# Scaling the softmax exponentials on VectorE instead of GpSimd, in a two-layer transformer block

## Chip, cores and metric

The kernel runs on one core of a Trainium2 chip. The metric is the device time of one execution in microseconds (us). The engines are TensorE (PE, with its weight loads as PEld), VectorE (DVE), ScalarE (ACT), GpSimd (POOL) and SyncE (SP, which issues nearly all DMAs). Each engine works through its own instructions in a fixed order; semaphores make one engine wait for another.

## What is computed

Two transformer layers on a sequence of 256 tokens with 1024 features, all in fp32. Each layer has a mixer with three kinds of attention (8 MLA heads, 4 "fox" heads with a forget-gate bias, 4 "moba" heads with a T5 bias) and a gated feed-forward part; both are modulated by columns computed from a condition vector.

```python
def dense_causal_attention(q, k, v, log_decay_cum=None):
    ...
        s = jnp.einsum('bhqd,bhkd->bhqk', q_i, k).astype(jnp.float32) * scale
        if log_decay_cum is not None:
            s = s + blk[2][..., None] - log_decay_cum[:, :, None, :]
        s = jnp.where(kpos[None, :] <= qpos[:, None], s, -jnp.inf)
        p = jax.nn.softmax(s, axis=-1)
        return jnp.einsum('bhqk,bhkd->bhqd', p.astype(v.dtype), v)

def reference(x, c, ...):
    c_act = jax.nn.silu(c)
    for l in range(DEPTH):
        mod = (c_act @ w_ada[l] + b_ada[l])[:, None, :]
        shift_a, scale_a, gate_a, shift_f, scale_f, gate_f = jnp.split(mod, 6, axis=-1)
        h = rmsnorm(x, g_mix_pre[l]) * (1.0 + scale_a) + shift_a
        y = hybrid_mixer(h, w_in[l], ..., g_group[l], w_out[l], t5_table)
        x = x + gate_a * rmsnorm(y, g_mix_post[l])
        h = rmsnorm(x, g_ffn_pre[l]) * (1.0 + scale_f) + shift_f
        x = x + gate_f * rmsnorm(swiglu(h, w_gate_up[l], w_down[l]), g_ffn_post[l])
    return x
```

## The kernel before, in words

Tokens lie on partitions in two tiles of 128, or on the free axis after a transpose. Every weight matrix streams from HBM in fp32 and is split into a high part `wh` (ScalarE, line 107) and a remainder `wl` (VectorE, line 108); a product is three matmuls (lines 153 to 155 and 175 to 177). The modulation matrices `adaw` are used up chunk by chunk in between, some by TensorE (line 299), some by VectorE as a product with row `crow` and a sum (line 277); the SyncE queue loads the next chunk into a buffer when VectorE or TensorE has left it (4 buffers).

In the mixer the 16 heads come as 8 pairs: four MLA pairs, two fox pairs, two moba pairs. For a pair TensorE computes the scores `s` (lines 500 and 502, one PSUM tile for each head), then for each head `softmax` runs. VectorE adds the mask or bias and takes the row minimum of the negated scores, once for the first 128 queries (128 keys, line 477) and once for the second (256 keys, line 479), into tile `e` of 128 x 384. ScalarE takes the two exponentials and their sums (lines 482 and 483). VectorE takes the reciprocals of the two sums (line 485). GpSimd multiplies the two parts of `e` by them (lines 486 and 487). Then TensorE transposes the three blocks of `e` into `pt` (line 493), ScalarE copies them to `pts` (line 495), and TensorE forms the head outputs `o` (line 521). A pair's transposes and outputs are issued one pair later for MLA and two pairs later for fox and moba (`DEPTH`), with projections and modulation chunks in between.

Each of the three groups then needs the sum of its squared outputs: `acc` is added on VectorE (line 527), summed over partitions by TensorE into `st` (line 461), turned into a factor on ScalarE (lines 463 and 464), applied on VectorE as `ov` (line 538), and split into `oH` and `oL`. The output projection `y` (lines 175 to 177, 96 matmuls a layer) takes `oH` and `oL` of eight 128-row pieces, the MLA pieces first and the moba pieces last. Its accumulators come from the same four PSUM buffers as the scores:

```python
def pa(name, n=512):
    return psum.tile([P, n], F32, tag="pa", bufs=4, name=name)
```

so `y` of the first token tile takes the buffers that the scores of the first moba pair held, and that of the second token tile those of the second moba pair. After `y` a norm follows (lines 385 to 454), then transposes `xT` (line 423) and the feed-forward part, whose matmuls are most of the time.

The order of the instructions on each engine is made by a scheduler of the framework from the code, with its own estimate of what each instruction takes. So a change in one line can move other instructions on all engines.

## Time and profile before

| | us |
|---|---|
| median of 3 runs | 661.24 (659.17 to 662.15) |
| the profiled execution, whole | 659.96 |
| its span, from the first to the last instruction | 658.2 |
| TensorE busy in the span | 630.1 |
| VectorE busy | 452.2 |
| ScalarE busy | 366.3 |
| GpSimd busy | 58.7 |

The granted clock of TensorE was 0.999 of full speed over the span. The two mixers with their attention lie at about 60 to 142 us and 353 to 450 us of the span; the feed-forward parts follow each of them. A row of the time line gives an instruction's start and duration, and in brackets how long its engine had been idle before it and what ended that; a row of the waits gives the sum, the count and the longest. Instructions of one engine overlap a little: the next one may start before the last one is recorded as over.

### The profile page before, as it was taken

What the parts mean: (1) busy time and instruction counts of PE and PEld (TensorE: products, weight loads), DVE (VectorE), ACT (ScalarE), POOL (GpSimd) and SP (SyncE); (2) the same over time, 40 slices, a digit from 0 to 9 for tenths busy, and PEclk for the clock granted to TensorE, in tenths of its full rate; (3) what the DMA queues carried; (4) which work ended last, traced back from release to release, by engine and by line L of the source; (5) the groups of instructions that cost most, each with busy time, mean ns of one, the idle gap of its engine ahead of it and who ended that gap; (6) DMA issues with size and microseconds to landing.
All of it is one profiled execution on the core that took longest, in us unless ns stands there. A gap on an engine that the chain in (4) does not pass through costs nothing.

```text
span 658.2 us, 11876 instructions
## 1 busy us (share of the span) xinstructions
PE 630.1 (96%) x4469; PEld 558.3 (85%) x4469; DVE 452.2 (69%) x892; ACT 366.3 (56%) x760; POOL 58.7 (9%) x95
## 2 busy tenths in 40 slices
PE   7998989999999999999999999999999999999996
PEld 5888776678999999999978997667999999999994
DVE  3878568878777777795668665957867854555443
ACT  5467577777644444444477765877754444444431
POOL 2000134400000000000011031420000000000000
PEclk9999999999999999999999999999999999999999
DMA  8988979654788998998834776724378665555511
GB/s 315 402 320 290 312 250 319 226 188 157 238 279 307 333 296 312 306 338 308 286 132 134 260 256 192 257 97 134 127 262 305 196 222 176 183 189 188 182 47 64
DMA packets 43337, 154.46 MB, mean 235 GB/s; under 512 B 5052, under 2 KB 5248, under 8 KB 43280
## 3 DMA queue, kind: packets, MB, share of 16 engines
q1 hardware_dynamic: 43008, 153.07, 68.1%
q8 instruction: 35, 0.57, 0.3%
q0 software_dynamic: 272, 0.63, 0.3%
q14 instruction: 22, 0.18, 0.1%
HBM read 152.60 MB, written 1.08 MB: 233 GB/s over the span
## 4 chain that ended last, share of the span: by engine, by line
PE 74%; DMA 10%; DVE 7%; ACT 3%; issue 2%; POOL 2%; SPq 1%; DVEq 0%; POOLq 0%; ACTq 0%
PE gu L153 11%; PE gu L154 11%; PE gu L155 11%; PE y L177 8%; PE y L175 8%; PE y L176 8%; DMA adaw<-in_w_ada_dram 5%; DVE wl L108 3%; PE o L521 2%; DMA raw_a<-in_w_a_dram 2%; DMA raw_b<-in_w_b_dram 2%; POOL rs L386 1%; PE pt L493 1%; ACT wh L107 1%; DVE x L454 1%
## 5 line engine op out<-in xcount | busy, mean ns | idle before, releaser
L108 DVE TENSOR_TENSOR wl<-raw_gu,wh 128x1024 fp32r<-128x1024 f32 (+1 forms) x100 | 108.5, 1095 | 70.3 <-ACT wh L107 69.9
L107 ACT ACTIVATE wh<-raw_gu 128x1024 fp32r<-128x1024 f32 (+1 forms) x100 | 94.3, 957 | 92.3 <-PE gu L154 66.7
L277 DVE CUSTOM_DVE_ANT_0 adaw<-adaw,crow 128x1024 f32<-128x1024 f32 x64 | 77.6, 1227 | 15.0 <-DMA adaw<-in_w_ada_dram 14.9
L153 PE MATMUL gu<-h0fL,wh 128*128 128x256 f32 x304 | 86.1, 283 | 0.0
L153 PE MATMUL gu<-h1fL,wh 128*128 128x256 f32 x304 | 86.1, 283 | 0.0
L154 PE MATMUL gu<-h1fH,wh 128*128 128x256 f32 x304 | 86.1, 283 | 0.0
L154 PE MATMUL gu<-h0fH,wh 128*128 128x256 f32 x304 | 86.0, 283 | 0.0
L155 PE MATMUL gu<-h1fH,wl 128*128 128x256 f32 x304 | 86.0, 283 | 0.0
L155 PE MATMUL gu<-h0fH,wl 128*128 128x256 f32 x304 | 85.9, 283 | 0.0
L107 ACT ACTIVATE wh<-raw_dn 128x1024 fp32r<-128x1024 f32 x44 | 46.6, 1060 | 57.5 <-issue 36.4
L108 DVE TENSOR_TENSOR wl<-raw_dn,wh 128x1024 fp32r<-128x1024 f32 x44 | 53.7, 1223 | 24.7 <-ACT wh L107 24.5
L176 PE MATMUL y<-wh,hid 128*128 128x512 f32 x176 | 69.6, 395 | 0.0
L175 PE MATMUL y<-wh,hid 128*128 128x512 f32 x176 | 69.5, 396 | 0.0
L177 PE MATMUL y<-wl,hid 128*128 128x512 f32 x176 | 69.5, 395 | 0.0
L154 PEld LDWEIGHTS gu<-h1fH,wh 128*128 128x128 f32 x304 | 58.2, 192 | 0.4
L154 PEld LDWEIGHTS gu<-h0fH,wh 128*128 128x128 f32 x304 | 58.2, 192 | 0.4
L153 PEld LDWEIGHTS gu<-h1fL,wh 128*128 128x128 f32 x304 | 58.2, 192 | 0.4
L153 PEld LDWEIGHTS gu<-h0fL,wh 128*128 128x128 f32 x304 | 58.2, 192 | 0.4
L155 PEld LDWEIGHTS gu<-h1fH,wl 128*128 128x128 f32 x304 | 58.2, 192 | 0.0
L155 PEld LDWEIGHTS gu<-h0fH,wl 128*128 128x128 f32 x304 | 58.2, 192 | 0.0
L386 POOL TENSOR_TENSOR rs<-rs,mhalf 128x1 f32<-128x1 f32 x16 | 11.1, 691 | 438.2 <-DVE rs L385 438.2
L177 PEld LDWEIGHTS y<-wl,hid 128*128 128x128 f32 x176 | 33.0, 188 | 8.0
(343 smaller groups left out, 1464.6 us busy)
## 6 DMA issues: line engine op xcount, KB each, us to landing
adaw<-in_w_ada_dram SPq DMA_DIRECT2D x96, 512.0 KB, 5.7
raw_gu<-in_w_gu_dram SPq DMA_DIRECT2D x88, 512.0 KB, 5.0
raw_dn<-in_w_dn_dram SPq DMA_DIRECT2D x44, 512.0 KB, 4.7
raw_out<-in_w_out_dram SPq DMA_DIRECT2D x16, 512.0 KB, 6.3
raw_b<-in_w_b_dram SPq DMA_DIRECT2D x12, 512.0 KB, 4.9
raw_a<-in_w_a_dram SPq DMA_DIRECT2D x8, 448.0 KB, 9.8
raw_uq<-in_w_uq_dram SPq DMA_DIRECT2D x4, 512.0 KB, 4.9
raw_vm<-in_w_vm_dram SPq DMA_DIRECT2D x4, 512.0 KB, 5.1
```

The lines of the kernel that those rows point to most:

```text
L107: ACT.activation(dst_h, src, AF.Copy)
L108: return DVE.tensor_tensor(dst_l, src, dst_h.bitcast(F32), op=ALU.subtract)
L153: chain(PE.matmul(ps, w[0], x[1], start=start, stop=False))
L154: chain(PE.matmul(ps, w[0], x[0], start=False, stop=False))
L155: chain(PE.matmul(ps, w[1], x[0], start=False, stop=stop))
L175: PE.matmul(ps, x[1], w[0], start=start, stop=False)
L176: PE.matmul(ps, x[0], w[0], start=False, stop=False)
L177: PE.matmul(ps, x[0], w[1], start=False, stop=stop)
L277: i = DVE.tensor_tensor_reduce(out=raws[u], in0=raws[u], in1=crow, op0=ALU.mult, op1=ALU.add, scale=1.0, scalar=0.0, accum_out=dst[:, u:u ...
L386: POOL.tensor_tensor(r, r, mhalf, op=ALU.pow)
L454: DVE.scalar_tensor_tensor(x[:, t, sl], ygs[n], r, x[:, t, sl], op0=ALU.mult, op1=ALU.add)
L521: PE.matmul(o[64 * u:64 * u + 64, lo:lo + n], v[:, u * 64:(u + 1) * 64], ps[u][:, i * P:i * P + n], start=i == 0, stop=i == 2, tile_positi ...
```

## The change

The two multiplications of each head go from GpSimd to VectorE, directly behind the reciprocal in the code. The tile, its parts and the factor stay as they are; the second multiplication by 1.0 inside the instruction goes.

```diff
         ri = wk.tile([P, 2], F32, tag="ri", bufs=4, name="ri")
         DVE.reciprocal(ri, sm)
-        POOL.tensor_scalar(e[:, 0:P], e[:, 0:P], ri[:, 0:1], 1.0, op0=ALU.mult, op1=ALU.mult)
-        POOL.tensor_scalar(e[:, P:3 * P], e[:, P:3 * P], ri[:, 1:2], 1.0, op0=ALU.mult, op1=ALU.mult)
+        for t, sl in ((0, slice(0, P)), (1, slice(P, 3 * P))):
+            DVE.tensor_scalar(e[:, sl], e[:, sl], ri[:, t:t + 1], None, op0=ALU.mult)
         return e
```

There are 32 heads in the two layers, so 64 instructions leave GpSimd's queue and 64 join VectorE's. They don't always stand directly behind their reciprocal there, and the scheduler has put other instructions into another order, on TensorE and ScalarE too. Three places follow.

VectorE in layer 0, second MLA pair, second head: from its reciprocal (tile `ri_1048`, of the exponentials `e_1041`) to the queries `qx_1121` of the third MLA pair. Before:

```order
L485 RECIPROCAL ri_1048<-sm_1045 128x2
L277 ISA adaw_1098,gcol_887<-adaw_1098,crow_110 128x1024
L277 ISA gcol_887 128x1
L108 TENSOR_TENSOR wl_826<-raw_out_823,wh_825 128x1024
L277 ISA adaw_1099,gcol_887<-adaw_1099,crow_110 128x1024
L277 ISA gcol_887 128x1
L806 TENSOR_TENSOR qx_1121<-qp_1120,qt_648 128x512
```

After:

```order
L277 ISA adaw_1098,gcol_887<-adaw_1098,crow_110 128x1024
L277 ISA gcol_887 128x1
L108 TENSOR_TENSOR wl_826<-raw_out_823,wh_825 128x1024
L485 RECIPROCAL ri_1048<-sm_1045 128x2
L277 ISA adaw_1099,gcol_887<-adaw_1099,crow_110 128x1024
L277 ISA gcol_887 128x1
L487 TENSOR_SCALAR e_1041<-e_1041,ri_1048 128x128
L487 TENSOR_SCALAR e_1041<-e_1041,ri_1048 128x256
L354 TENSOR_TENSOR gcol_887<-gcol_887,first_73 128x8
L806 TENSOR_TENSOR qx_1121<-qp_1120,qt_648 128x512
```

The reciprocal now stands behind one modulation chunk (`adaw_1098`) and one weight split, and another chunk (`adaw_1099`) stands between it and the two scalings; `qx` comes behind all of them.

VectorE in layer 0, around the reciprocals of the second fox pair (`acc<-acc,osq` is the sum of squares of the MLA group, `ov<-oc` its outputs, `e,mn<-s,mobab` the minima of the first moba pair). Before:

```order
L277 ISA adaw,ab_1221<-adaw,crow 128x1024
L277 ISA ab_1221 128x1
L485 RECIPROCAL ri<-sm 128x2 x2
L326 TENSOR_TENSOR ab_1221<-ab_1221,first 128x8
L477 ISA e,mn<-s,mobab 128x128
L477 ISA mn 128x1
L527 TENSOR_TENSOR acc<-acc,osq 128x256
L328 SCALAR_TENSOR_TENSOR ab_1221<-ab_1221,first 128x4
L479 ISA e,mn<-s,mobab 128x256
L479 ISA mn 128x1
```

After:

```order
L527 TENSOR_TENSOR acc<-acc,osq 128x256
L277 ISA adaw,ab_1221<-adaw,crow 128x1024
L277 ISA ab_1221 128x1
L485 RECIPROCAL ri<-sm 128x2 x2
L277 ISA adaw,ab_1221<-adaw,crow 128x1024
L277 ISA ab_1221 128x1
L487 TENSOR_SCALAR e<-e,ri 128x128
L487 TENSOR_SCALAR e<-e,ri 128x256
L487 TENSOR_SCALAR e<-e,ri 128x128
L487 TENSOR_SCALAR e<-e,ri 128x256
L538 SCALAR_TENSOR_TENSOR ov<-oc,first,ocr 128x256 x2
L326 TENSOR_TENSOR ab_1221<-ab_1221,first 128x8
```

The sum of squares moved ahead of both chunks of line 277 (the first of them stood before the minima of the second fox pair until now), and the minima of the first moba pair moved behind the first two `ov`.

VectorE in layer 1, around the minima of the second moba pair, the last softmax of the mixer. Before:

```order
L538 SCALAR_TENSOR_TENSOR ov<-oc,first,ocr 128x256 x2
L326 TENSOR_TENSOR ab_4479<-ab_4479,first 128x8
L485 RECIPROCAL ri<-sm 128x2
L108 TENSOR_TENSOR o1L<-ov,o1H 128x256
L328 SCALAR_TENSOR_TENSOR ab_4479<-ab_4479,first 128x4
L477 ISA e,mn<-s,mobab 128x128
L477 ISA mn 128x1
L479 ISA e,mn<-s,mobab 128x256
L479 ISA mn 128x1
```

After:

```order
L538 SCALAR_TENSOR_TENSOR ov<-oc,first,ocr 128x256 x2
L487 TENSOR_SCALAR e<-e,ri 128x128
L108 TENSOR_TENSOR o1L<-ov,o1H 128x256
L487 TENSOR_SCALAR e<-e,ri 128x256
L277 ISA adaw,ab_4479<-adaw,crow 128x1024
L277 ISA ab_4479 128x1
L108 TENSOR_TENSOR o1L<-ov,o1H 128x256
L326 TENSOR_TENSOR ab_4479<-ab_4479,first 128x8
L477 ISA e,mn<-s,mobab 128x128
L477 ISA mn 128x1
L328 SCALAR_TENSOR_TENSOR ab_4479<-ab_4479,first 128x4
L479 ISA e,mn<-s,mobab 128x256
```

A modulation chunk that stood further ahead now stands with the two scalings in front of these minima, and both heads' minima of the pair follow behind it.

## Rows read from the trace of the kernel before

**Rows 1.** The page, busy time of each engine (share of the span), xinstructions.

```profile
PE 630.1 (96%) x4469; PEld 558.3 (85%) x4469; DVE 452.2 (69%) x892; ACT 366.3 (56%) x760; POOL 58.7 (9%) x95
```

**Rows 2.** Busy us by stretch: length, then PE, PEld, DVE, ACT, POOL; clock, DMA.

```profile
100.00:120.00 20.00, 17.91 (x157) 11.19 (x156) 17.88 (x71) 16.14 (x57) 10.34 (x16) 1.00 0.94 324
410.00:430.00 20.00, 17.56 (x145) 11.67 (x146) 19.48 (x69) 17.82 (x57) 9.72 (x17) 1.00 0.70 246
430.00:442.00 12.00, 12.00 (x68) 8.31 (x67) 5.48 (x20) 8.77 (x27) 1.71 (x4) 1.00 0.29 91
```

**Rows 3.** Lines 486 and 487: busy us, mean ns, idle before; then ns min/median/max.

```profile
L487 POOL TENSOR_SCALAR e<-e,ri 128x256 f32<-128x256 f32 x32 | 21.8, 682 | 0.0
L486 POOL TENSOR_SCALAR e<-e,ri 128x128 f32<-128x128 f32 x32 | 21.2, 662 | 134.2 <-DVE ri L485 123.2 <-PE qkp L155 6.5 <-DVE ab L326 3.9
...
L486 POOL TENSOR_SCALAR e<-e,ri x32: 366/372/2388, 73.0 to 433.7; 128x128 f32<-128x128 f32 x32
L487 POOL TENSOR_SCALAR e<-e,ri x32: 468/480/1513, 73.4 to 434.0; 128x256 f32<-128x256 f32 x32
```

**Rows 4.** Groups of VectorE, shapes apart; then two neighbours of line 420 in time.

```profile
L404 DVE TENSOR_SCALAR diag<-first,rs 128x128 f32<-128x128 f32 x2 | 0.6, 282 | 0.6 <-POOL rs L386 0.6
L420 DVE TENSOR_SCALAR xn<-x,rs 128x512 f32<-128x512 f32 x12 | 5.3, 483 | 2.7 <-POOL rs L386 2.7
...
146.60 0.88 DVE L420 TENSOR_SCALAR xn<-x,rs 128x512 f32<-128x512 f32 x2 [0.44 <-POOL rs L386]
```

**Rows 5.** Waits of PE (us, times, longest): first 60 to 140, then 380 to 450.

```profile
PE pt L493 <- POOL e L486: 2.2, 2, 1.7
PE pt L493 <- POOL e L487: 1.1, 1, 1.1
PE st L461 <- DVE acc L527: 1.1, 1, 1.1
PE y L175 <- DVE o0L L108: 0.6, 1, 0.6
...
PE s L500 <- DVE qx L806: 1.6, 2, 1.3
PE pt L493 <- POOL e L487: 0.2, 1, 0.2
```

**Rows 6.** Time line of layer 0's second and third MLA pair: start us, us.

```profile
84.38 0.17 DVE L485 RECIPROCAL ri<-sm 128x2 f32<-128x2 f32 x1 [0.71 <-ACT e L483]
84.50 1.23 DVE L277 CUSTOM_DVE_ANT_0 adaw<-adaw,crow 128x1024 f32<-128x1024 f32 x1
84.64 2.39 POOL L486 TENSOR_SCALAR e<-e,ri 128x128 f32<-128x128 f32 x1 [0.52 <-DVE ri L485]
...
85.65 1.22 DVE L108 TENSOR_TENSOR wl<-raw_out,wh 128x1024 fp32r<-128x1024 f32 x1
...
87.08 0.33 PE L493 MATMUL pt<-first,e 128*128 128x128 f32 x1 [1.71 <-POOL e L486]
...
88.03 0.68 DVE L806 TENSOR_TENSOR qx<-qp,qt 128x512 f32<-128x512 f32 x1
88.50 0.20 PEld L493 LDWEIGHTS pt<-first,e 128*128 128x128 f32 x2 [1.28 <-POOL e L487]
...
88.86 0.68 PE L500 MATMUL s<-kx,qx 128*128 128x128 f32 x4
```

**Rows 7.** Time line of layer 0's fox and moba pairs.

```profile
110.02 1.23 DVE L277 CUSTOM_DVE_ANT_0 adaw<-adaw,crow 128x1024 f32<-128x1024 f32 x1 [1.21 <-DMA adaw<-in_w_ada_dram]
...
113.96 0.52 DVE L527 TENSOR_TENSOR acc<-acc,osq 128x256 f32<-128x256 f32 x1
...
119.05 0.64 POOL L487 TENSOR_SCALAR e<-e,ri 128x256 f32<-128x256 f32 x1
```

**Rows 8.** Time line of layer 1's last moba head.

```profile
434.03 0.48 POOL L487 TENSOR_SCALAR e<-e,ri 128x256 f32<-128x256 f32 x1
```

## The prediction

> **What bounds the kernel now.** I read the busy times first. TensorE is busy for 630.1 of 658.2 us [rows 1], so the change can give back only what TensorE waits, 28 us over the whole span, and only in the two mixers, since no scaling lies elsewhere. The stretches of the mixers come next [rows 2]: with both fox and moba groups in flight TensorE is idle for 2.1 us of 100 to 120 and 2.4 us of 410 to 430. VectorE, which is to get the work, is busy there for 17.88 and for 19.48 of 20 us. From 430 to 442 TensorE has no gap at all (12.00 of 12) and VectorE is half idle. Third, the waits of TensorE [rows 5]: for GpSimd's two scalings it waited 2.2 + 1.1 us in layer 0 and 0.2 us in layer 1, 3.5 us together; for VectorE 1.1 us (the sum of squares `acc`), 0.6 us (`o0L`) and 1.6 us (`qx`). So GpSimd holds TensorE up for 0.5% of the time, and VectorE, the engine that gets the work, for nearly as much.
>
> **What is removed.** GpSimd is busy for 21.2 + 21.8 = 43.0 us with the 64 scalings; at their medians they would take 32 x (0.372 + 0.480) = 27.3 us, so 15.7 us are stretching [rows 3]. The longest shows what it is: started at 84.64, it took 2.39 us and ended as VectorE's chunk (84.50) and weight split (85.65, 1.22 us) were over [rows 6]. None of the 43 us counts in itself; GpSimd's queue holds hardly anything else here. What counts is the 3.5 us for which TensorE waited.
>
> **What is added.** VectorE's multiplication by a column took 282 ns for 128 columns and 483 ns for 512; on that line 256 columns take 282 + 201 x 128/384 = 349 ns. Two neighbours of 512 took 0.88 us together, 0.09 less than 2 x 0.483, so each hides 0.09 us under the next [rows 4]. A head costs VectorE's queue 0.19 + 0.26, rounded 0.46 us; 32 heads 14.7 us. Bounds: 0.63 us a head if nothing overlaps (20.2 us), and 0.31 if both parts ran at the slope alone plus one start. I take 0.46, since the neighbours are the same operation on the same engine.
>
> [...]
>
> The 14.7 us lie where VectorE has room, or before somebody who waits. Three places decide.
>
> **Place 1, layer 0, second MLA pair.** TensorE waits here 1.71 us and then about 1.1 us for the second head's scaling, the bulk of the 3.5 us [rows 5, 6]. But the scores behind it start at 88.86, and `qx`, which they need, ends on VectorE at 88.03 + 0.68 = 88.71. Had GpSimd been done at once, TensorE would have waited for `qx` all the same. Now the scalings come into that very queue. The order puts the chunk and the weight split ahead of the reciprocal and one more chunk between it and the scalings; `qx` stays last. What VectorE does until `qx` grows by two heads, 0.92 us, and loses the 0.71 us for which it waited in front of the reciprocal at 84.38, since the exponential is done by the time it comes to it. Term: +0.2 us. Bounds: -2.8 us if both waits really go, +1.4 us if a chunk of 1.23 us [rows 6] has to wait for its data in front.
>
> **Place 2, layer 0, fox and moba.** The chunk at 110.02 had waited 1.21 us for its transfer and then ran 1.23 us, with the minima of the second fox pair queued behind it [rows 7]. Now four heads' scalings, 1.84 us, are done before it, which mostly fills VectorE's idle time (2.1 us of 100 to 120, rows 2), and these minima and `acc` stand in front of the chunk. `acc`, at 113.96 before, then comes up to two chunks earlier, and TensorE's waits of 1.1 us for it and 0.6 us for `o0L` can go: -1.7 us. Against this, the first moba pair's minima now stand behind two chunks, four scalings and two `ov`, and its last scaling, which ended at 119.05 + 0.64 = 119.69 [rows 7], comes later by the four heads' 1.84 us, with a chunk of 1.23 us 3.1 us. While this lasts, `y` of the first token tile can't begin, as its accumulators are these scores' buffers. Term: -1.0 us, nearer to the gain, since TensorE has the second fox pair's transposes and outputs to do meanwhile. Bounds: -1.7 and 3.1 - 1.7 = +1.4 us.
>
> **Place 3, layer 1, fox and moba.** In 410 to 430 GpSimd ran 17 instructions, the scalings of eight heads: 8 x 0.46 = 3.7 us for a VectorE with 0.5 us free [rows 2]. So VectorE ends this stretch about 3.2 us later, and the last moba scaling, over at 434.03 + 0.48 = 434.51 [rows 8], comes at about 437.7. What hides it is `y`: 72 of its 96 matmuls need no moba output, and TensorE's 68 matmuls of 430 to 442 took 12.00 us, 0.18 us each [rows 2], so 18 of them cover 3.2 us. The new order does put more of them ahead of the last pair. Before 430 there is no `y` to fill with; there a late `acc` or transpose shows at once. Term: +0.6 us, a fifth of the lateness. Bounds: 0 and +3.2 us.
>
> **Sum.** +0.2 - 1.0 + 0.6 = -0.2 us. The profiled execution took 659.96 us (span 658.2, 1.8 us outside it), so it becomes 659.8; it lay 1.3 us below the median of the runs, and on the median of 661.24 the same change gives 661.0.
>
> **Rivals.** *The waits go, faster.* If the stretching of GpSimd is the cause and VectorE brings its own scalings in time, all of the 3.5 us of TensorE's waits for GpSimd come back [rows 5]: 657.7 us; with place 2's 1.7 us as well 656.0. For it: the stretched scalings at 84.64, and that place 2 starts earlier. Against it: `qx` ends last at place 1. [...] Chance 0.2.
>
> *VectorE becomes the bound, slower.* Place 3's 3.2 us are not covered, because the late transposes and sums of squares come before there is any `y`, and place 1 adds its 0.2: 661.24 + 3.4 = 664.6 us. It decides from the point at which the second moba pair's transposes come to TensorE's head before their scaling is done. For it: 19.48 of 20 us busy. Against it: `y` matmuls without need for them, and 6.5 us of idle VectorE right behind [rows 2]. Chance 0.2.
>
> *The waits change their owner* is the forecast, 659.5 to 662.7 us, chance 0.6.
>
> **How the numbers follow.** The likeliest case gives 661.0. The range takes in the first rival at 657.7 and the second at 664.6, and leaves out the rest of both: 657.5 to 664.9. A measurement of this kernel can tell about 0.5%, 3.3 us: below 657.9 lies a little more than half of the first rival, 0.13; above 664.5 half of the second and an uncovered place 2 beside it, 0.15; within, 0.72.
>
> **What would show it.** The waits for lines 486 and 487 are gone in any case. Right: VectorE busy longer by 15 to 20 us; scores of the third MLA pair still at 88.7 to 89.3 with a wait of TensorE near 3 us in front of them, now for VectorE; `st` of the MLA group in layer 0 a microsecond or two earlier; the last moba scaling of layer 1 three us later with TensorE busy beside it. Wrong: the scores well before 88.5 (first rival), or gaps of TensorE between 420 and 435 that sum to over 3 us (second rival). A scaling that takes VectorE much more than 0.35 us would upset places 1 and 3 alike.

## The result, and the profile after

The changed kernel takes 665.12 us (median of 6 runs, 662.96 to 670.59) against 661.52 us for the kernel before beside it (6 runs, 659.17 to 662.44): 1.0061 of it, with a 95% interval of 1.0035 to 1.0088. It is slower by 0.6%, and the time lies 0.2 us above the predicted range. Repeated later it took 667.13 us, 1.0065 [1.0040, 1.0091]. The profiled execution took 662.96 us with a span of 661.2.

The page of the kernel after, busy time of each engine, as [rows 1]:

```profile
PE 632.6 (96%) x4469; PEld 560.2 (85%) x4469; DVE 464.3 (70%) x956; ACT 366.5 (55%) x760; POOL 16.6 (3%) x31
```

GpSimd has lost its 64 instructions and 42 us, and VectorE has taken them, but it is busy for only 12.1 us more. The busy times by stretch, as [rows 2] (length, PE, PEld, DVE, ACT, POOL, clock, DMA):

```profile
100.00:120.00 20.00, 19.16 (x159) 12.07 (x158) 18.16 (x71) 15.18 (x51) 0.00 (x0) 1.00 0.87 285
410.00:430.00 20.00, 16.60 (x133) 11.65 (x136) 18.46 (x71) 16.09 (x50) 0.00 (x0) 1.00 0.60 205
430.00:442.00 12.00, 11.83 (x76) 7.40 (x69) 10.25 (x36) 9.49 (x31) 0.00 (x0) 1.00 0.51 176
```

In layer 0 TensorE is now busy for 19.16 of 20 us (17.91 before), in layer 1 for 16.60 (17.56 before). Of the scalings themselves, the groups of the new line 487 (busy us, mean ns, idle before):

```profile
L487 DVE TENSOR_SCALAR e<-e,ri 128x256 f32<-128x256 f32 x32 | 11.1, 348 | 0.0
L487 DVE TENSOR_SCALAR e<-e,ri 128x128 f32<-128x128 f32 x32 | 9.1, 283 | 0.3
```

283 and 348 ns are the 282 of [rows 4] and the 349 that were worked out from them. The waits of TensorE, as [rows 5], from 60 to 140 and then from 380 to 450 us:

```profile
PE pt L493 <- DVE e L487: 2.1, 1, 2.1
PE s L500 <- DVE qx L806: 0.9, 1, 0.9
PE o L521 <- ACT pts L495: 0.7, 1, 0.7
...
PE s L500 <- DVE qx L806: 1.1, 1, 1.1
PE pt L493 <- ACT e L483: 1.0, 1, 1.0
PE o L521 <- ACT pts L495: 0.8, 2, 0.4
PE st L461 <- DVE acc L527: 0.6, 1, 0.6
```

The 3.3 us of waits for GpSimd in layer 0 have become 2.1 us for VectorE, the waits for `acc` and `o0L` there are gone, and one for `acc` and one for a transpose stand in layer 1, where none was. These waits alone do not add up to the loss. For that the span is cut into four stretches, each from the first matmul of one kind to that of another:

- **A**, layer 0, from the scores of the first MLA pair to those of the third (the prediction's place 1);
- **B**, from there to the first `gut` of the feed-forward (place 2);
- **C**, layer 1, from the scores of the first MLA pair to those of the last;
- **D**, from there to the first `gut` of layer 1's feed-forward (place 3).

What lies between B and C took 228.4 to 228.7 us in all kernels below but three (e6, e12 and e13, 229.4 to 229.5, where the clock fell once on the way), what lies behind D 197.0 to 197.5. The start, up to A, took 69.4 to 71.6, with no scaling in it. The table has each kernel's median and its ratio to the kernel before on the same chip (worked out from all runs of both, so it is not the quotient of two medians), and the four stretches of its profiled execution in us; for B and D the granted clock stands in brackets where it is under 1.00. In A it was 0.98 in e2 and 0.94 in e15. One execution of the kernel before beside e1 to e4, 688.88 us at a clock of 0.849, is left out everywhere.

| kernel | scalings on VectorE | median | ratio [95%] | A | B | C | D |
|---|---|---|---|---|---|---|---|
| before | none | 661.52 | | 19.44 | 61.89 | 32.49 | 49.32 |
| after | all | 665.12 | 1.0061 [1.0035, 1.0088] | 18.01 | 63.57 (.97) | 32.10 | 51.88 |
| e1_same | none (kernel before) | 662.43 | 1.0021 [0.9994, 1.0047] | 18.23 | 62.92 (.97) | 33.43 | 50.82 (.97) |
| e2_layer0 | layer 0 | 663.56 | 1.0027 [1.0005, 1.0048] | 19.32 | 63.24 (.98) | 33.35 | 49.77 |
| e3_layer1 | layer 1 | 665.25 | 1.0040 [1.0016, 1.0064] | 17.92 | 63.28 (.97) | 32.62 | 53.13 (.97) |
| e4_mla | MLA heads | 663.28 | 1.0040 [1.0012, 1.0068] | 17.78 | 60.46 | 32.96 | 53.10 (.97) |
| e5_four | 4 heads | 665.15 | 1.0055 [1.0032, 1.0078] | 18.77 | 62.89 (.97) | 32.53 | 53.55 (.97) |
| e6_allbut | all but these 4 | 664.00 | 1.0064 [1.0034, 1.0094] | 18.59 | 63.52 (.97) | 34.13 | 51.39 (.97) |
| e7_late | all, in front of the transposes | 670.16 | 1.0125 [1.0082, 1.0168] | 20.38 | 66.12 (.98) | 33.97 | 52.72 |
| e8_none | no scaling at all | 660.46 | 0.9989 [0.9969, 1.0008] | 18.39 | 63.40 (.97) | 32.20 | 50.58 (.97) |
| e9_fox0 | 2 heads, first fox pair | 664.62 | 1.0030 [1.0013, 1.0048] | 17.32 | 61.73 | 33.53 | 54.14 (.94) |
| e10_mla3 | 2 heads, last MLA pair | 665.66 | 1.0063 [1.0036, 1.0090] | 18.19 | 61.83 | 32.79 | 53.08 (.97) |
| e11_qx | none; `qx` earlier | 658.16 | 0.9932 [0.9906, 0.9958] | 15.84 | 60.95 | 31.84 | 49.31 |
| e12_qx_dve | all; `qx` earlier | 663.94 | 1.0021 [1.0001, 1.0041] | 16.57 | 63.95 | 32.86 | 51.87 |
| e13_thin4 | all, of 4 heads 4 columns a part | 666.44 | 1.0063 [1.0036, 1.0089] | 18.35 | 63.52 (.97) | 32.04 | 52.28 (.97) |
| e14_thick4 | none; dummies for 4 heads | 665.31 | 1.0050 [1.0029, 1.0070] | 18.14 | 61.91 | 33.41 | 53.79 (.97) |
| e15_after | all | 667.13 | 1.0065 [1.0040, 1.0091] | 19.29 | 63.99 (.96) | 34.50 | 51.93 |
| e16_allbut2 | all but 4 heads | 666.87 | 1.0053 [1.0027, 1.0079] | 18.49 | 64.11 (.97) | 34.09 | 51.16 (.97) |
| e17_four2 | 4 heads | 666.03 | 1.0050 [1.0029, 1.0072] | 18.08 | 61.34 | 33.71 | 53.41 (.97) |
| e18_thin32 | all, 4 columns a part | 662.71 | 1.0011 [0.9990, 1.0031] | 18.61 | 61.54 (.98) | 32.21 | 50.76 |

Two things have to be taken out before rows are compared. The kernel before itself shows D at 49.32 us with the clock at 1.00 throughout and at 50.82 where it fell once (e1); by this one pair a fall is taken as 1.5 us there. In B it shows 61.89 and 62.92. And C contains a wait for a transfer that has nothing to do with the change. Here is the kernel after, in both its profiled executions: VectorE's chunk ahead of the minima of the third MLA pair; first the execution whose stretches stand under after, then e15:

```profile
404.92 1.23 DVE L277 CUSTOM_DVE_ANT_0 adaw<-adaw,crow 128x1024 f32<-128x1024 f32 x1 [1.77 <-DMA adaw<-in_w_ada_dram]
```

```profile
408.50 1.23 DVE L277 CUSTOM_DVE_ANT_0 adaw<-adaw,crow 128x1024 f32<-128x1024 f32 x1 [4.19 <-DMA adaw<-in_w_ada_dram]
```

C took 32.10 and 34.50: less the 1.77 and the 4.19, both times 30.3. Done so for every kernel, C is 29.70 +- 0.02 wherever GpSimd scales layer 1's MLA heads ahead of the last pair (before, e1, e2, e5, e9, e10, e11, e14, e17) and 30.32 +- 0.02 wherever VectorE does so in full (after, e3, e4, e6, e7, e12, e13, e15, e16); 29.58 without any scaling and with all of them thin.

So the loss by stretch, like with like: **A** none that stands out (17.3 to 19.4 with GpSimd, 17.8 to 19.3 with VectorE, means 18.3 and 18.5; e7, e8, e18 and the `qx` kernels aside), **B** about +0.6 (with a fall 62.89 to 63.28 for GpSimd in e1, e3 and e5, 63.24 to 64.11 for VectorE in after, e2, e6, e13, e15 and e16, means 63.0 and 63.7), **C** +0.6, **D** +2.6 (51.88, 51.93 and 51.87 against 49.32 and 49.31, all without a fall; against the 49.77 of e2, whose layer 1 is GpSimd's too, +2.1). Together 3.8 us, or 3.3 with e2's D, where the medians differ by 3.6 and the ratio's interval is 2.3 to 5.8 us. The size of B is the least certain: without a fall there is only e12 with all scalings on VectorE, 63.95, against 61.34 to 61.91 for GpSimd, and the kernel with no scaling at all (e8) has 63.40 with a fall, as much as with VectorE.

Where D loses is seen in the time line (start us, us, instruction, idle before and its releaser). The kernel before, around the minima of the second fox pair and the sum of squares of the MLA group:

```profile
422.54 0.28 DVE L477 CUSTOM_DVE_ANT_0 e<-s,fb 128x128 f32<-128x128 f32 x1
...
422.87 0.40 ACT L482 ACTIVATE e<-e,mn 128x128 f32<-128x128 f32 x1
...
424.63 0.36 ACT L523 ACTIVATE oc<-o 128x256 f32<-128x256 f32 x1
...
425.29 0.41 ACT L525 ACTIVATE osq<-oc 128x256 f32<-128x256 f32 x1
425.73 0.48 DVE L527 TENSOR_TENSOR acc<-acc,osq 128x256 f32<-128x256 f32 x1
425.93 0.55 PE L493 MATMUL pt<-first,e 128*128 128x128 f32 x3
426.31 0.66 PE L461 MATMUL st<-acc,shp 128*128 128x256 f32 x2
```

The kernel after, the same place, and its last moba scaling:

```profile
424.50 0.29 DVE L477 CUSTOM_DVE_ANT_0 e<-s,fb 128x128 f32<-128x128 f32 x1
...
424.93 0.38 ACT L523 ACTIVATE oc<-o 128x256 f32<-128x256 f32 x1 [0.95 <-PE o L521]
...
425.85 0.39 ACT L482 ACTIVATE e<-e,mn 128x128 f32<-128x128 f32 x1
...
427.26 0.55 DVE L487 TENSOR_SCALAR e<-e,ri 128x128 f32<-128x128 f32 x2
427.60 0.40 ACT L525 ACTIVATE osq<-oc 128x256 f32<-128x256 f32 x1
427.69 0.61 PE L493 MATMUL pt<-first,e 128*128 128x128 f32 x3 [1.02 <-ACT e L483]
428.47 0.42 DVE L527 TENSOR_TENSOR acc<-acc,osq 128x256 f32<-128x256 f32 x1
428.94 0.48 PE L461 MATMUL st<-acc,shp 128*128 128x256 f32 x1 [0.64 <-DVE acc L527]
...
438.88 0.55 DVE L487 TENSOR_SCALAR e<-e,ri 128x128 f32<-128x128 f32 x2
```

D starts 0.38 us later here (412.21 against 411.83), and the minima of the second fox pair 1.96 us later: by then VectorE has done the scalings of the last MLA pair and of the first fox pair, four heads at 0.46 us, 1.8 us, in front of them. The pair's exponentials come 2.98 us later (422.87 and 425.85). Only 1.96 of that is the minima's lateness: the other 1.02 us are the order of ScalarE's queue, where the copy `oc`, which stood behind these exponentials, now stands in front of them and waits 0.95 us for `o`. From there the lateness goes on to TensorE, which waits 1.02 us for the transposes' operand; ScalarE comes to the square `osq` 2.3 us later, and `acc` with it, for which TensorE waits 0.64 us. TensorE's idle time in D grows from 49.32 - 46.88 = 2.44 to 51.88 - 47.98 = 3.90 us; for the other 1.1 us the same 288 matmuls show more busy time, most of it in `y` and in the moba pairs' outputs, and why is not shown. All this lies before the first `y`, which starts at 432.44. Of D's 2.56 us, 1.80 stand by then (20.23 against 18.43 us from D's start), and 0.76 come behind it.

### The profile page after: what moved, and what is told of

It is laid out like the page before. It is cut to its first block, busy times and chain, and to the rows that moved or that the text cites. A ratio compares the mean times of both kernels' runs of the same rounds, so it can differ in the third digit from the quotient of the medians.

```text
span 661.2 us, 11822 instructions
## 1 busy us (share of the span) xinstructions
PE 632.6 (96%) x4469; PEld 560.2 (85%) x4469; DVE 464.3 (70%) x956; ACT 366.5 (55%) x760; POOL 16.6 (3%) x31
## 4 chain that ended last, share of the span: by engine, by line
PE 79%; DVE 7%; ACT 6%; DMA 4%; issue 2%; POOL 1%; SPq 0%; DVEq 0%; POOLq 0%; ACTq 0%
PE gu L153 11%; PE gu L154 11%; PE gu L155 11%; PE y L175 8%; PE y L177 8%; PE y L176 8%; DMA adaw<-in_w_ada_dram 3%; PE o L521 2%; DVE wl L108 2%; ACT wh L107 1%; PE qkp L153 1%; PE qkp L155 1%; PE qkp L154 1%; POOL rs L386 1%; ACT hv L427 1%
## 5 line engine op out<-in xcount | busy, mean ns | idle before, releaser
L175 PEld LDWEIGHTS y<-wh,hid 128*128 128x128 f32 x176 | 33.1, 188 | 7.4 <-DVE hid L108 0.3
```

Source lines behind the costliest of these rows:

```text
L175: PE.matmul(ps, x[1], w[0], start=start, stop=False)
```

## The experiments

**The same again, and half of the change.** e1 is the kernel before, unchanged.

> The kernel before, unchanged, to see the granted clock of each of its runs. Theory A (the loss lies in the order of VectorE in layer 1, where the scalings put the second fox pair's minima back, plus a fall of the clock at the second MLA pair of layer 0): ratio 1.000 within 0.003, granted clock 0.998 to 0.999 in nearly all runs, since without the long single wait of TensorE at 85 to 87 us the clock does not fall. Theory B (the loss is a matter of runs, whose clock also falls now and then at the start, in front of any scaling): clocks between 0.98 and 0.995 here as often as with the change, and the times follow them.

Measured: 1.0021, so with the same code the comparison itself can be 0.2% off. Its clock was 0.988 to 0.996 over the runs, and not the 0.999 of the profiled execution before; so theory A was wrong about the clock, which falls with the kernel before too. The stretches B and D show a fall each that the kernel before did not have when it was profiled. What the profiled execution of the kernel before shows is therefore its form without a fall.

e2, e3 and e4, and below e5, e6, e9, e10, e16 and e17, have one edit; only the condition differs, here for e2 (e3: `l == 1`; e4: True for MLA, False for fox and moba):

```diff
-    def softmax(s, b0, b1):
+    def softmax(s, b0, b1, dve):
...
-        POOL.tensor_scalar(e[:, 0:P], e[:, 0:P], ri[:, 0:1], 1.0, op0=ALU.mult, op1=ALU.mult)
-        POOL.tensor_scalar(e[:, P:3 * P], e[:, P:3 * P], ri[:, 1:2], 1.0, op0=ALU.mult, op1=ALU.mult)
+        for t, sl in ((0, slice(0, P)), (1, slice(P, 3 * P))):
+            (DVE if dve else POOL).tensor_scalar(e[:, sl], e[:, sl], ri[:, t:t + 1], None if dve else 1.0, op0=ALU.mult, **({} if dve else {"op1": ALU.mult}))
...
-            es = [softmax(ss[u], mask[:, P:S], mask) for u in range(2)]
+            es = [softmax(ss[u], mask[:, P:S], mask, l == 0) for u in range(2)]
```

> The scalings of layer 0 go to VectorE, those of layer 1 stay on GpSimd. Theory A: the 2.3 us that layer 1 lost between 420 and 429 us are not there; the scores of the third MLA pair of layer 0 start about 1.5 us earlier than before and the clock falls behind them, which takes about as much back: 661.0 to 662.5 us, ratio 0.999 to 1.002, clock near 0.996. Theory B: no difference that can be told from the kernel before, and clocks like those of the kernel before.

> The scalings of layer 1 go to VectorE, those of layer 0 stay on GpSimd. Theory A: the sum of squares of the MLA group in layer 1 comes 2 to 2.7 us late and the whole time grows by 2 to 2.5 us: 663.4 to 664.0 us, ratio 1.003 to 1.004, clock 0.999 as before. Theory B: ratio 1.000, and the 2.3 us are given back by y and the norm behind it.

> The scalings of the eight MLA heads of each layer go to VectorE, those of the fox and moba heads stay on GpSimd. Theory A: at the fox pairs of layer 1 VectorE has only two scaled heads more than before in front of the second fox pair's minima instead of four or more, so about 0.5 to 1.0 us of the 2.3 us stay; layer 0 as with the whole change: 661.5 to 663.0 us. Theory B: within 0.2% of the kernel before, with clocks like its own.

Measured: layer 0 alone 1.0027, hardly more than the same code, where theory A had at most 1.002; layer 1 alone 1.0040 with D at 53.13 against 50.82, both with a fall; the MLA heads alone 1.0040, with the best B of all kernels that leave `qx` where it was (60.46, 1.4 under the kernel before) and a D that loses 2.3 us (53.10 against 50.82) where theory A had 0.5 to 1.0. The whole times of the two layers can't be told apart, their intervals overlap; by the stretches the larger loss is layer 1's, and the one profiled execution of e4 shows a gain in layer 0 that is gone when the fox and moba heads move as well.

**Which heads.** e5 moves four heads of layer 1 alone (last MLA pair, first fox pair: the ones ahead of the minima at 422.54); e6 moves all but these. Conditions `l == 1 and hp == 3` and `l == 1 and i == 0 and hp == 0`, and their negation. e9 and e10 move two heads each. e16 and e17 repeat e6 and e5 side by side.

> Only four heads of layer 1 are scaled by VectorE, the two of the last MLA pair and the two of the first fox pair, whose scalings stand in VectorE's queue in front of the second fox pair's minima; the other 28 heads stay on GpSimd. Theory A (these four heads, 4 x 0.46 us, put the minima back, and with them the exponentials, the transposes and the sum of squares of the MLA group, for which TensorE then waits): as much loss as with all of layer 1, 2.0 to 2.6 us, ratio 1.003 to 1.004; from the scores of the last MLA pair of layer 1 to the start of the next feed-forward part 51.3 to 52 us where before took 49.3, if the clock does not fall within. Rival C (it is the sum of VectorE's work in the layer, 16 heads x 0.46 = 7.4 us, that counts): a quarter of the loss, 0.6 us, and 49.9 us for that stretch.

> The opposite: 28 heads are scaled by VectorE, only the four heads of layer 1 (last MLA pair, first fox pair) stay on GpSimd. Theory A: the stretch from the scores of the last MLA pair to the next feed-forward part takes 49.0 to 50.0 us as before, and the whole time is that of the kernel before to within 0.2%, 661 to 662.5 us. Rival C: three quarters of the loss in layer 1 stay, 1.7 us, 51.0 us for the stretch and 663 to 664 us in all.

> Only two heads are scaled by VectorE, those of the first fox pair of layer 1; 30 heads stay on GpSimd. Theory A, now: the loss in layer 1 goes with the scalings that stand in front of the second fox pair's minima. Two heads put them back by 0.9 us instead of four by 1.8: 0.6 to 1.6 us of loss, 50.0 to 51.0 us from the last MLA scores to the feed-forward part at full clock, ratio 1.001 to 1.0025. Rival D (it is not the time of the scalings but the new order around them, in which the MLA group's sum of squares stands behind the exponentials of the fox pairs): no loss, 49.0 to 49.6 us, if the sum of squares stands early, as it does here, ahead of all the moba pairs' minima.

> Only two heads are scaled by VectorE, those of the last MLA pair of layer 1. Theory A: they too stand in front of the fox pairs' minima, so again 0.6 to 1.6 us, 50.0 to 51.0 us for the stretch, ratio 1.001 to 1.0025. Rival D: the order puts the sum of squares of the MLA group behind a modulation chunk of 1.2 us and behind the first moba pair's minima; the loss is that of the whole change, 2 us or more, and the wait of TensorE is for the sum of squares.

> The sixth kernel again (VectorE scales all heads but the last MLA pair and the first fox pair of layer 1), since its whole time did not fit its stretches: it was 3.4 us above the kernel before although the stretch of layer 1 from the last MLA pair's scores to the feed-forward had only 0.5 us more at full clock. If the loss sits in these four heads' stretch alone, the repeated run is 0 to 1.5 us above the kernel before, and the 3.4 us were executions with more falls of the clock (its mean was 0.989 against 0.9925). If every group of scalings on VectorE brings a loss of its own and the losses do not add, it is 2 to 4 us above again, at the same mean clock as the kernel before.

> The fifth kernel again (VectorE scales only those four heads), on the same chip as its complement. If the loss sits in these four heads alone: 3 to 4.5 us above the kernel before, and at least 1.5 us above the complement. If the losses do not add: both are about the same, 2 to 4 us above. In both cases the stretch of layer 1 takes 51.5 to 52.5 us at full clock here and 49.3 to 50.2 us in the complement.

Measured: D with the four heads alone is 53.55 and 53.41, 2.6 to 2.7 above the 50.82 of e1, all with one fall; without them 51.39 and 51.16, 0.3 to 0.6 above. So these four heads are enough for the loss of D. In whole time, though, e6 and e16 lose as much (1.0064, 1.0053) as e5 and e17 (1.0055, 1.0050): the losses of the parts do not add up to that of the whole, and the reading after e5 that the four heads make nearly all of the loss was wrong. What e6 and e16 lose is B's 0.6, C's 0.6 and D's 0.3 to 0.6, some 1.7 us. Part of the rest is the clock: its mean was 0.9893 and 0.9901 over their runs, against 0.9925 and 0.9913 for the kernel before beside them, by the slope in the last section an estimate of 1.4 and 0.5 us; what is left is of the size that the same code showed in e1.

The two heads of e9 and of e10 show that D is not proportional to the heads. e10 has 53.08, 2.3 above e1, for two heads; e9, whose stretch had two falls, about 1.8 when 1.5 are taken off for each; theory A had 1.6 at most for either. And the wait is another one each time. TensorE's waits in e9, then in e10:

```profile
PE o L521 <- ACT pts L495: 1.6, 2, 1.4
```

```profile
PE st L461 <- DVE acc L527: 2.1, 1, 2.1
```

In e9 TensorE waits for ScalarE's copies `pts`, which start at 431.83 behind exponentials and the split `o1H` in ScalarE's queue, although the transposes that they copy were done at 427.4. In e5 and e17 it waits 1.0 us in D for scalings that stayed on GpSimd. In e10 `acc` comes behind a modulation chunk in VectorE's queue; that is what rival D had forecast for e10, a loss of 2 us or more by the order, with the wait for the sum of squares.

**Later in the program, and not at all.** e7 writes the scaling, on VectorE, in front of the transposes instead of behind the reciprocal. e8 leaves the scaling out.

```diff
-        POOL.tensor_scalar(e[:, 0:P], e[:, 0:P], ri[:, 0:1], 1.0, op0=ALU.mult, op1=ALU.mult)
-        POOL.tensor_scalar(e[:, P:3 * P], e[:, P:3 * P], ri[:, 1:2], 1.0, op0=ALU.mult, op1=ALU.mult)
-        return e
+        return e, ri
...
+        e, ri = e
+        for t, sl in ((0, slice(0, P)), (1, slice(P, 3 * P))):
+            DVE.tensor_scalar(e[:, sl], e[:, sl], ri[:, t:t + 1], None, op0=ALU.mult)
```

> All scalings on VectorE, but written where the transposes are issued, one or two pairs later, instead of behind the reciprocal; in layer 1 only the last MLA pair's two heads then stand in front of the second fox pair's minima, not four. Theory A: about half of the loss in layer 1 is left, 0.9 to 1.4 us, 50.2 to 50.8 us for the stretch from the last MLA scores to the feed-forward part; in all 661.5 to 663.0 us, ratio 1.000 to 1.002. Rival C: as with the whole change, 1.004 to 1.006.

> Nobody scales: the exponentials go to the transposes as they are (this part of the computation is left out), so TensorE never waits for a scaling. It prices what a perfect change could give. Theory A, by which the queries of the third MLA pair end last at the first place: the scores there start at most 0.5 us earlier against the start of the first MLA pair's scores than with GpSimd (17.9 to 19.4 us), and the whole time falls by 0 to 1.5 us, 660.2 to 661.7 us, ratio 0.998 to 1.000. The rival by which all of TensorE's waits for GpSimd come back, 3.5 us: 658.2 us, ratio 0.995.

Measured: e7 1.0125, twice the loss and outside what either theory had: A, B and D are all longer. e8 0.9989: **with no scaling on any engine the kernel is not measurably faster.** By the interval GpSimd's scalings cost the kernel before 0.3% at most, 2 us, for all their 43 us [rows 3] and the 3.5 us of waits [rows 5]; leaving them out orders the queues anew too. The time line of e8 at place 1 tells why:

```profile
88.49 0.68 DVE L804 TENSOR_TENSOR qx<-qp,qt 128x512 f32<-128x512 f32 x1
...
89.32 0.72 PE L498 MATMUL s<-kx,qx 128*128 128x128 f32 x4 [3.10 <-DVE gcol L354]
```

With nothing to scale, TensorE does its transposes at once and then waits 3.10 us until `qx` has ended on VectorE (88.49 + 0.68 = 89.17). The row names `gcol`, but the scores read `qx`, and they start 0.15 us behind its end here as in the kernel before (88.71 and 88.86).

**What TensorE does wait for at place 1.** e11 is the kernel before with `qx` of layer 0's third MLA pair ahead of the two modulation chunks; e12 has the same and all scalings on VectorE.

```diff
+                if last.get("hold"):
+                    order_after(i, last["qx"])
...
-            DVE.tensor_tensor(qx, qp.rearrange("p (u s) -> p u s", u=2),
+            last["qx"] = DVE.tensor_tensor(qx, qp.rearrange("p (u s) -> p u s", u=2),
...
+            if l == 0 and hp == 2:
+                last["hold"] = True
+                fill()
+                last["hold"] = False
...
-            fill()
+            if l or i != 1: fill()
```

> The scalings stay on GpSimd as before; what changes is layer 0's third MLA pair: the two modulation chunks that stood in front of its queries in VectorE's queue are put behind them. If these queries are what TensorE waits for at that place, as the run without any scaling says (the same stretch there), the scores of the third MLA pair come 1.2 to 2.4 us earlier against the first pair's (16 to 17.5 us instead of 18 to 19.4), the clock does not fall behind them, and the whole time falls by 1 to 3 us: 658 to 660.5 us, ratio 0.9955 to 0.9985. If the place is bound by something else (the key copies, the transfer), nothing changes.

> The same move of the two chunks, with all scalings on VectorE as in the changed kernel. If the loss of the changed kernel lies in layer 1 alone, this is the gain of the move against the changed kernel: 662 to 664 us, ratio to the kernel before 1.001 to 1.004, with the scores of the third MLA pair again 16 to 17.5 us behind the first pair's.

Measured: e11 658.16 us, 0.9932 [0.9906, 0.9958], **faster than both kernels**; e12 1.0021. The time line of e11 at place 1:

```profile
84.35 0.37 POOL L488 TENSOR_SCALAR e<-e,ri 128x128 f32<-128x128 f32 x1 [0.58 <-DVE ri L487]
...
86.26 0.68 DVE L808 TENSOR_TENSOR qx<-qp,qt 128x512 f32<-128x512 f32 x1
86.86 1.22 DVE L277 CUSTOM_DVE_ANT_0 adaw<-adaw,crow 128x1024 f32<-128x1024 f32 x1
87.08 0.68 PE L502 MATMUL s<-kx,qx 128*128 128x128 f32 x4 [0.55 <-DVE qx L808]
```

`qx` now precedes a chunk, A takes 15.84 us, and GpSimd's scaling of 2.39 us [rows 6] takes 0.37, the median of [rows 3]. e12 against e11 is the change once more, with place 1 mended: 5.8 us between the medians. In the profiled executions, 8.2 us apart, B has 3.0 of it (63.95 against 60.95, neither with a fall), D 2.6, A 0.7, C without its transfer 0.6, and what lies between B and C 1.1. The 1.1 us are a fall of the clock that e12 has there and e11 has not (the mean clock of the two executions was 0.991 and 0.994). Whether the move costs more with place 1 mended is not shown: C and D lose what they lost before, and the interval of the first comparison reaches 5.8 us.

**Time, dependence or order.** In e13 all is as after, but the four heads' scalings go over 4 columns of each part (the rest stays unscaled). In e14 GpSimd scales as before, and VectorE multiplies into a tile that nobody reads wherever it would scale for the four heads. In e18 all scalings are on VectorE over 4 columns (the rest stays unscaled). e15 is the kernel after again.

```diff
+            DVE.tensor_scalar(e[:, sl][:, :4 if thin else None], e[:, sl][:, :4 if thin else None], ri[:, t:t + 1], None, op0=ALU.mult)
```

```diff
+        if busy:
+            d = wk.tile([P, 384], F32, tag="busy", bufs=1, name="busy")
+            DVE.tensor_scalar(d[:, 0:P], mask[:, P:S], ri[:, 0:1], None, op0=ALU.mult)
+            DVE.tensor_scalar(d[:, P:3 * P], mask, ri[:, 1:2], None, op0=ALU.mult)
```

> The changed kernel, with the scalings of the four heads (last MLA pair and first fox pair of layer 1) cut to 4 columns in each part, so that they stand in VectorE's queue and hold hardly any time there; the other columns of these heads stay unscaled. If the time of these scalings makes the loss, the stretch from the last MLA scores to the feed-forward part falls from 51.9 to 49.3 to 50.2 us at full clock, as with these heads on GpSimd (50.0). If it is that they stand there at all and what order comes of it, it stays at 51 to 52 us. In all 662 to 663 us against 664 to 665.

> The kernel before, all scalings on GpSimd, with two more instructions of VectorE for each of the same four heads: multiplications of 128x128 and 128x256 into a tile that nobody reads, in the places where the scalings would stand. VectorE's queue is then that of the run with these four heads on VectorE, but no transpose waits for it. If VectorE's queue makes the loss, 51.3 to 52.2 us for the stretch at full clock and ratio 1.003 to 1.0055; if it is the wait of the transposes for a scaling in VectorE's queue, 49.3 to 50.0 us and ratio 1.000 to 1.001.

> The changed kernel again, beside the same runs of the kernel before, for a second trace of it: 51.5 to 52.2 us for the stretch at full clock, ratio 1.004 to 1.008.

> All 64 scalings on VectorE, but each over 4 columns only, so that the rest of the exponentials stays unscaled (left out): the instructions and their waits are in VectorE's queue, their time is nearly gone; about 64 x 0.1 us of it should be left. If the time of the scalings makes the loss, this takes what the kernel without any scaling took, which was equal to the kernel before: within 1 us of the kernel before. If the instructions' places in the queue, and the order that comes with them, make it: 2 to 4 us above the kernel before, as the changed kernel.

Measured: e14 has the loss of D in full (53.79, 3.0 above e1) although no transpose depends on VectorE's multiplications: so the new dependence of TensorE on VectorE is not needed for it, and what VectorE's queue holds, with the order that comes with it, is enough. e13 keeps 52.28 - 50.82 = 1.5 of 2.6 us in D, e18 50.76 - 49.32 = 1.4 (each compared with the kernel that has as many falls); in both TensorE waits 1.7 us for `acc`. Thin does not mean without time; the one line of e18 (ns min, median, max):

```profile
L487 DVE TENSOR_SCALAR e<-e,ri x64: 217/226/232, 72.6 to 435.7; 128x4 f32<-128x4 f32 x64
```

226 ns for 4 columns, and two such take VectorE 0.26 us (one starts at 418.57, the instruction behind the second at 418.83), where a full head takes 0.46. So 0.26/0.46 = 57% of the time was left, and 1.4 to 1.5 of 2.6 us, 54 to 58%, of D's loss. That agrees with a loss that goes by the time of the scalings in the queue; that two heads cost 1.8 to 2.3 does not, so the order which comes with each edit has its share. In whole time e18 is 1.0011, no loss that can be told: its B is 61.54 even with the clock falling, and its C 29.58 without the transfer. Each of these edits changes the order of the queues as well. That of ScalarE is the plainest: in all ten kernels in which VectorE has such work for the first fox pair (after, e3, e5, e9, e12 to e15, e17 and e18) `oc` waits its 0.95 us in front of the second fox pair's exponentials, which start 0.89 to 1.36 us behind their minima; in the other ten they start 0.33 to 0.67 us behind. No kernel here has the order of after without the time of the scalings, or the time without the order; how the 2.6 us divide between the two stays open.

## Why the prediction was wrong

**Right: the bound and the price of a scaling.** The step that TensorE's waits are all there is to gain, and that the waits for GpSimd would not come back since `qx` ends last at place 1, is shown by e8 and e11. That refutes the first rival (656.0 to 657.7 us) at its root. The stretching itself is there and ends with the change: in the kernel before GpSimd's scalings of 128 columns took 0.37 us at the median [rows 3], but 1.21 to 2.39 us where a chunk of VectorE ran beside them for over 1 us (five of the 32), and VectorE's `ov` of the MLA groups, 471 to 694 ns with a median of 580, take 476 to 485 with a median of 478 in the kernel after. But no time that can be told comes back with it: e8, without any scaling, is at 0.9989. The price was right too: two heads' four scalings start at 408.52 and the next instruction at 409.45, 0.46 us a head, as predicted. (Its lower bound of 0.31 us does not follow from the rows named: 384 columns at the slope and one start are 0.20 + 0.215 = 0.42 us; nothing rests on it.) VectorE is busy longer by 12.1 us, not 15 to 20: the scalings add 13.8 and its other instructions take 1.7 less, `ov` alone 0.9.

**Place 1, predicted +0.2 us (A): right, as far as it can be told.** Scores at 88.16, a little ahead of the 88.7 to 89.3 that was named, with TensorE's wait of 2.09 us for the scaling in front of them. In the time line of after:

```profile
85.66 1.21 DVE L277 CUSTOM_DVE_ANT_0 adaw<-adaw,crow 128x1024 f32<-128x1024 f32 x1
86.79 0.55 DVE L487 TENSOR_SCALAR e<-e,ri 128x128 f32<-128x128 f32 x2
87.22 0.61 PE L493 MATMUL pt<-first,e 128*128 128x128 f32 x3 [2.09 <-DVE e L487]
87.32 0.69 DVE L806 TENSOR_TENSOR qx<-qp,qt 128x512 f32<-128x512 f32 x1
88.16 0.46 PE L500 MATMUL s<-kx,qx 128*128 128x128 f32 x2 [0.33 <-DVE gcol L355]
```

The wait has changed its owner and `qx` stands right behind, as said. The length of A varies between executions by more than the term (19.44 and 18.23 with the same code).

**Place 2, predicted -1.0 us (B): wrong in sign, +0.6.** The gain came as described: in the time line of after,

```profile
113.12 0.43 DVE L527 TENSOR_TENSOR acc<-acc,osq 128x256 f32<-128x256 f32 x1 [1.00 <-ACT osq L525]
113.61 0.70 PE L461 MATMUL st<-acc,shp 128*128 128x256 f32 x2
...
120.84 0.50 PE L175 MATMUL y<-wh,o0L 128*128 128x512 f32 x1
```

`acc` is 0.84 us earlier than the 113.96 of [rows 7], the waits for it and for `o0L` are gone, and e4 has the gain by itself (-1.4). But the price named beside it, the later moba pairs in front of `y`, took it back and more. Here e1 is the kernel to compare with, since its scores start at 88.14 with a fall behind them, as here at 88.16. First e1's first `y` and its start of the feed-forward, then the latter in after:

```profile
119.32 0.50 PE L175 MATMUL y<-wh,o0L 128*128 128x512 f32 x1 [0.63 <-DVE o0L L108]
...
151.06 0.39 PE L168 MATMUL gut<-wh,h0fH 128*128 128x256 f32 x1 [0.59 <-DVE h0fH L429]
```

```profile
151.73 0.38 PE L168 MATMUL gut<-wh,h0fH 128*128 128x256 f32 x1 [1.75 <-DVE h0fH L429]
```

The first `y` starts 1.52 us later than in e1. TensorE does other work meanwhile and does not wait there, so far as predicted; but the norm of the first token tile, which needs its `y`, comes 0.6 to 1.1 us later (its first square starts at 140.75 against 140.19, its last factor `rs` at 146.80 against 145.68), while TensorE ends its `y` 0.6 us earlier. So it has nothing left to do in front of `gut` and waits 1.75 us for its operand, 1.16 more than in e1. The step that failed was "nearer to the gain, since TensorE has the second fox pair's transposes and outputs to do meanwhile": that work covered the late start of `y`, and not its late end for the first tile, which was not priced. The value lies inside the bounds that were given, -1.7 and +1.4.

**Place 3, predicted +0.6 us (D): 2.6, the step that decides.** The last moba scaling ended at 439.43 (437.7 predicted), and what was said of its cover held: from 430 to 442 TensorE is busy for 11.83 of 12 us. The failed step is "+0.6, a fifth of the lateness": the lateness was counted only at its end, behind the first `y`, where it is hidden. It arises 15 us sooner, at the second fox pair, with four heads' scalings ahead of its minima, where TensorE has no `y` to fill with. The sentence on this stood in the prediction ("before 430 there is no `y` to fill with") but had no price; four heads by 0.46, 1.8 us, was to be had from its own numbers. ScalarE's new order there, another 1.02 us for the exponentials, was not in the prediction at all.

**Not in the sum: C, +0.6.** It lies between the scores of the first and of the second MLA pair of layer 1, 10.81 us instead of 10.09. The kernel before, then after, from `qx` to the second pair's scores:

```profile
388.59 0.69 DVE L806 TENSOR_TENSOR qx<-qp,shp 128x512 f32<-128x512 f32 x1
...
389.42 0.68 PE L500 MATMUL s<-kx,qx 128*128 128x128 f32 x4 [0.24 <-DVE qx L806]
```

```profile
389.40 0.69 DVE L806 TENSOR_TENSOR qx<-qp,shp 128x512 f32<-128x512 f32 x1
...
390.35 0.65 PE L521 MATMUL o<-pts,vc 128*64 128x256 f32 x2 [0.40 <-ACT pts L495]
390.93 0.71 PE L500 MATMUL s<-kx,qx 128*128 128x128 f32 x4
```

Counted from C's start, `qx` ends as before (9.94 and 9.97 us). What is new is TensorE's own order: two outputs `o` of the first pair, with a wait of 0.40 us for `pts`, stand in front of the scores. They stand there in all nine kernels with 30.32 us and in none of the others. So this part of the loss is the new order of the queues, and not VectorE's time.

**The rival that came true.** The second rival's 664.6 us is near the 665.12, with D as its main loss as it said. Its deciding point was wrong: the second moba pair's transposes, covered by `y`, do not hold TensorE up; those of the second fox pair do. TensorE's gaps between 420 and 435 sum to 2.3 us (0.8 before), not to over 3, and VectorE is no fuller than before in 410 to 430, 18.46 us against 19.48: it stands idle for 0.94 us at 426.85 until the late exponentials end. So the rows show a delay handed on through VectorE and ScalarE, more than VectorE's load. That the measured time lies near the rival's is in part luck, since B and C, which it did not have, bring 1.2 us of the loss. As sums: predicted 0.2 - 1.0 + 0.6 = -0.2, measured 0 + 0.6 + 0.6 + 2.6 = 3.8.

## What to carry to other kernels

Before pricing a move of work off a slow engine, find what the consumer would wait for if that work were free; where another operand ends last, as `qx` here, the move gains nothing there, and putting that operand ahead of filler work in its queue (e11, -0.7%) is worth more than the move. Count what a move adds to a nearly full queue at the first instruction behind it that feeds the bounding engine, not at the last one, and ask at that point what the bounding engine has to do meanwhile. Compare the new order on every engine, not only on the one that gets the work: C's loss came with the order of TensorE's queue, and part of the delay in D with that of ScalarE's. And measure parts of a change by stretches, not by whole times alone: a stretch shows which rows moved. Neither adds up here, though: two pairs of heads lose 1.8 and 2.3 us of D by themselves and 2.6 to 2.7 together.

## What the runs showed of the hardware that was not expected

**The clock varies between executions of the same code.** In 136 executions of the kernel before the mean granted clock was 0.984 to 0.999 and the time 657.2 to 666.1 us: 23 of them at 0.9885 or less took 664.0 us on the mean, 23 at 0.9945 or more 659.8, a slope of 0.43 us for each 0.001. Two microseconds of e1, the kernel before:

```profile
90.00:92.00 2.00, 2.00 (x10) 1.11 (x10) 1.08 (x8) 1.96 (x9) 0.71 (x2) 0.50 0.76 256
```

The same two in the profiled execution of before:

```profile
90.00:92.00 2.00, 2.00 (x17) 1.35 (x16) 1.37 (x9) 1.44 (x7) 0.08 (x1) 1.00 0.75 277
```

The granted clock is 0.50 of full speed there, and TensorE does 10 pieces where it did 17. The falls come at places that recur from kernel to kernel (near 90 and from 410 to 436 us among them), behind stretches in which TensorE had waited (2.09 us up to 87.22 in the kernel after, 1.42 us up to 432.36 in e9), but not behind each: in the profiled execution of before the waits ahead of 90 us were longer than in e1 (1.7 and 1.1 us against 0.6 and 1.1), and it had no fall. What decides it is open.

**A transfer's landing shifts by 2.4 us between executions.** The chunk of layer 1 waited 1.77 to 4.19 us for the same weights in two executions of the same kernel, 2.78 and 3.72 in two of the kernel before, and C followed to within 0.02 us. With the clock's falls, taken above as 1 to 1.5 us each, this is the larger part of what looks like a difference between two single profiles.
